# Cross-covariance attention: the V side moved one step further behind the attention

## The chip, the cores and the metric

The kernel runs on one core of a Trainium2 chip. The metric is device time in microseconds (us); a lower number is better. The kernel before was run five times: 131.57 to 134.93 us, median 132.96 us. One further execution was profiled; it took 131.79 us, and 130.0 us lie between its first and its last instruction (the span).

## The reference

Q, K and V have the shape 8 x 12 x 512 x 64 (batch, heads, sequence n, feature), float32. The attention is over features, not over the sequence, so each head has a 64 x 64 attention matrix:

```python
Q_norm = Q / (np.linalg.norm(Q, axis=-2, keepdims=True) + 1e-10)
K_norm = K / (np.linalg.norm(K, axis=-2, keepdims=True) + 1e-10)
attn = np.einsum('bhnd,bhne->bhde', Q_norm, K_norm)
attn = np.exp(attn - np.max(attn, axis=-1, keepdims=True))
attn = attn / (np.sum(attn, axis=-1, keepdims=True) + 1e-10)
return np.einsum('bhnd,bhde->bhne', V, attn).astype(np.float32)
```

## The kernel before, in words

The 96 heads are cut into 24 units of four heads (U = 24). For each unit Q and K are one transfer of 512 KB each (`load_qk`, L69 to L73). V comes in 12 transfers of 1024 KB, each for two units (`load_v`, L75 to L77). The output leaves in one transfer of 512 KB for each unit, the last unit in two halves (`store`, L79 and L80). All transfers are issued by SyncE, SP in the profile, on one queue, in the order in which the program names them.

One unit passes through these stages. VectorE (DVE) casts Q and K to bf16 side by side (`cast_q` L84, `cast_k` L87). TensorE (PE) makes their Gram matrix in 64 small matmuls (`grams` L103); it holds the product of Q and K and, on its diagonal, the squared norms. VectorE reads the norms (`norms` L115), GpSimd (POOL) takes the power of -1/2 (L120) and scales the part of K (`scale_k` L125), which ScalarE (ACT) copied out of PSUM before (`keep_kq` L108). PE transposes (`logits` L131), VectorE applies the norms of Q (`scale_q` L135), ScalarE takes the exponential (`exps` L139), VectorE divides by the row sums (`normalise` L143 to L147), and PE and ScalarE put the result into a second place as well (`doubled` L176 and L177).

The V side of unit v has three parts. `cast_v(v)` (L96) casts half of a V transfer to bf16, one half of that on ScalarE and the other on VectorE. `vtrans(v)` transposes it on PE (L155) and copies it out of PSUM on ScalarE (L159). `outs(v)` multiplies it by the attention matrix on PE (L188) and copies the product on ScalarE (L192). The last four units use `vtrans_f32` (L170, L171), which transposes V without a cast and shares the copies between ScalarE and VectorE.

The order is written out by hand, and the pools keep to it (`manual_schedule`). A loop over s = 0..23 runs steps. Step s names: the transfers of Q and K of unit s + 3, the V transfers and stores that fall due, `cast_v` for the units in `new`, `cast_q(s + 1)`, `normalise(s - 2)`, `grams(s)`, `norms(s)`, `keep_kq(s)`, `scale_k(s)`, `logits(s - 1)`, `scale_q(s - 1)`, `exps(s - 1)`, `cast_k(s + 1)`, `outs` for the units from n0 to n1, `doubled(s - 2)`, and last `vtrans` for the units in `new`. Each engine works its own instructions off in this order. `outs_by(s)` (L62 to L64) says how many units have had `outs` after step s; it sets the due times of all V work: V transfers are issued while fewer than (n1 + 5) // 2 have been, stores while fewer than n1 - 3 have been, and `new` reaches to n1 + 2. After the loop a tail runs the last six units: `vtrans_f32(u + 2)` and `outs(u)` for u = 18..23, with the rest of the attention of units 22 and 23 between them.

Buffers that matter: five for Q and K, four for V as it arrives (`vp`), three for V in bf16, ten for outputs, one PSUM buffer for the transposed V (`ps_v`), two for products (`ps_o`), and one for the Gram matrix, whose space is given to the tail's transposes once the loop is over.

Of the kernel before, what the change touches and what calls it, by code (L numbers as in the profile page):

```python
# [27 lines left out]
def kernel(  # L28
# [10 lines left out]
    U = B * H // HU  # L39
# [21 lines left out]

    def outs_by(s):  # L62

        return max(0, (s - 2) * 9 // 10)  # L64


    qf, kf, vf, vb, qkb, nsq, rq, kqs, sl, ex, vt, so, kq = ({} for _ in range(13))
# [7 lines left out]
    def load_v(w):  # L75
        vf[w] = vp.tile([128, 2 * R * D], F32, name="vf")
        nc.sync.dma_start(out=vf[w], in_=Vf[w])  # L77

    def store(u, g=slice(0, SV)):  # L79
        nc.sync.dma_start(out=Of[u][:, g], in_=so[u][:, g].rearrange("p s t d -> p s (t d)"))  # L80
# [8 lines left out]
    def cast_v(v):  # L89

        w, i = divmod(v, 2)
        if i == 0:
            vb[w] = vbp.tile([128, A, TP, 2 * D], BF16, name="vb")
        x = vf[w].rearrange("p (a t d) -> p a t d", a=A, d=2 * D)
        for t, copy in ((2 * i, nc.scalar.copy), (2 * i + 1, nc.vector.tensor_copy)):
            copy(vb[w][:, :, t], x[:, :, t])  # L96
# [52 lines left out]
    def vtrans(v):  # L149

        w, i = divmod(v, 2)
        ps = ps_v.tile([128, A, 2, 128], BF16, name="vps")
        for t in range(2):
            for a in range(A):
                nc.tensor.transpose(ps[:, a, t, :], vb[w][:, a, 2 * i + t, :], identb)  # L155

        if i == 0:
            vt[w] = vtp.tile([128, TP, 128, A], BF16, name="vt")
        nc.scalar.copy(vt[w][:, 2 * i:2 * i + 2], ps.rearrange("p a t c -> p t c a"))  # L159
# [19 lines left out]
    def outs(u, copies=(nc.scalar.copy, nc.scalar.copy)):  # L179
        s = so[u] = sop.tile([128, SV, TP, 2 * D], F32, name="so")  # L180
        a = abuf[u % len(abuf)]
        v = vt[u // 2][:, :, u % 2 * 64:(u % 2 + 1) * 64]
        for g in range(SV):
            po = ps_o.tile([128, TP, 2 * D], F32, name="po")
            for t in range(TP):
                for x in range(2):
                    h = 2 * g + x
                    nc.tensor.matmul(  # L188
                        po[MV * x:MV * (x + 1), t, :], v[:, t, NP * h:NP * (h + 1), :].rearrange("p c a -> p (c a)"),
                        a[:, h].rearrange("p a d -> p (a d)"), tile_position=(0, MV * x),  # L190
                    )
            copies[g](s[:, g], po)  # L192
# [21 lines left out]
    def clear(i):  # L214

        nc.scalar.copy(abuf[i].rearrange("p h a d -> p (h a d)"), zeros)
# [4 lines left out]
    def on(f, u):  # L221
        if 0 <= u < U:
            f(u)

    on(cast_q, 0)
    on(cast_k, 0)
    load_v(0)
    nv, nst, nt = 1, 0, 0
    for s in range(U):
        n0, n1 = outs_by(s - 1), outs_by(s)  # L230
        on(load_qk, s + LOAD_AHEAD)
        while nv < min(U, n1 + 5) // 2:
            load_v(nv)
            nv += 1
        while nst < n1 - 3:
            store(nst)
            nst += 1
        new = range(nt, n1 + 2) if s >= 1 else ()
        for v in new:
            cast_v(v)  # L240
        on(cast_q, s + 1)
        on(normalise, s - 2)
        on(grams, s)
        on(norms, s)
        on(keep_kq, s)
        on(scale_k, s)
        on(logits, s - 1)
        on(scale_q, s - 1)
        on(exps, s - 1)
        on(cast_k, s + 1)  # L250
        for v in range(n0, n1):
            outs(v)
        on(doubled, s - 2)
        if 6 <= s + 5 < len(abuf):
            clear(s + 5)
        for v in new:
            vtrans(v)
            nt = v + 1
# [59 lines left out]
```

## Time and profile before

| What | Value |
|---|---|
| median of 5 runs | 132.96 us (131.57 to 134.93) |
| profiled execution: time, span | 131.79 us, 130.0 us |
| mean granted PE clock | 0.835 of full speed |
| busy: PE, DVE, ACT, POOL | 89.7, 95.2, 91.5, 63.6 us |
| moved | 50.67 MB, mean 390 GB/s |
| from issue to landing: Q, K, V, output (median) | 11.5, 11.2, 12.6, 11.2 us |

The profile page gives each engine's busy time, the span in 40 slices of 3.25 us with a busy digit each, the queues, the chain of work that ended last, and groups of instructions. A line of the timeline gives an instruction's start and length in us, the engine, the source line, the operation and its operands, and in square brackets how long the engine sat idle before it and who released it. The table by stretch gives busy us and instruction counts of PE, its weight loads, DVE, ACT and POOL, then the granted PE clock, the share of the DMA engines and GB/s.

### The profile page before, as it was taken

How to read it: one execution, taken by the hardware profiler on the slowest of the kernel's cores; microseconds unless marked ns; L12 is line 12 of the kernel's file. 1: busy time of each engine (PE TensorE's matmuls, PEld its weight loads, DVE VectorE, ACT ScalarE, POOL GpSimd, SP SyncE). 2: the span in 40 equal slices, each digit the busy share in tenths (PEclk: the TensorE clock that was granted, in tenths of full speed). 3: DMA queues.
4: the chain of work that ended last, by engine and by line, in shares of the span. 5: the costliest groups of instructions: out<-in, count | busy, mean ns of one | idle time of the engine just before them, and what ended most of it. 6: DMA issues, size and time to landing. Idle time of an engine off the chain costs nothing.

```text
span 130.0 us, 5389 instructions
## 1 busy us (share of the span) xinstructions
PE 89.7 (69%) x2232; PEld 69.7 (54%) x2232; DVE 95.2 (73%) x366; ACT 91.5 (70%) x171; POOL 63.6 (49%) x57
## 2 busy tenths in 40 slices
PE   0147328479977759883995699765598499979640
PEld 0136226357855537662873587554486378767420
DVE  0450673989798995993978897997689597878840
ACT  7600373575999999895778387999489968887530
POOL 4005080895369753751738574579347627640000
PEclk9999999955599996897579856999959955999965
DMA  4999999999999999999999999999999999998775
GB/s 151 355 391 427 421 412 406 410 418 407 402 421 397 426 404 416 417 416 406 422 405 413 403 419 415 409 418 415 411 414 422 400 420 413 415 359 328 297 287 203
DMA packets 15208, 50.67 MB, mean 390 GB/s; under 512 B 1360, under 2 KB 1360, under 8 KB 13648
## 3 DMA queue, kind: packets, MB, share of 16 engines
q1 hardware_dynamic: 15184, 50.34, 97.1%
q8 instruction: 17, 0.28, 0.8%
q14 instruction: 7, 0.06, 0.1%
HBM read 37.75 MB, written 12.58 MB: 387 GB/s over the span
## 4 chain that ended last, share of the span: by engine, by line
PE 44%; ACT 14%; DVE 13%; issue 9%; DMA 8%; POOL 6%; SPq 2%; DVEq 0%; POOLq 0%; ACTq 0%
PE gram L103 17%; PE po L188 9%; DMA vf<-in_V_dram 8%; PE vps L155 7%; DVE scr L115 5%; POOL rq L120 5%; PE lgdup L131 4%; ACT vt L159 4%; ACT so L192 4%; PE lgdup L176 3%; PE vps L170 2%; DVE sl L135 2%; POOL kqs L125 1%; ACT kq L108 1%; DVE qkb L87 1%
## 5 line engine op out<-in xcount | busy, mean ns | idle before, releaser
L120 POOL TENSOR_TENSOR rq<-nsq,mhalf 128x4 f32<-128x4 f32 x24 | 47.4, 1975 | 49.7 <-DVE nsq L115 35.8
L103 PE MATMUL gram<-qkb 32*128 32x128 bf16 x1536 | 36.1, 256 | 16.8 <-DVE qkb L87 9.1
L103 PEld LDWEIGHTS <-qkb 32*128 32x128 bf16 x1536 | 29.7, 114 | 23.5 <-DVE qkb L87 12.1
L115 DVE CUSTOM_DVE_ANT_0 scr<-gram,ident 128x128 f32<-128x128 f32 x96 | 22.1, 284 | 13.1 <-PE gram L103 13.0
L192 ACT COPY so<-po 128x512 f32<-128x512 f32 x42 | 22.8, 588 | 1.6 <-PE po L188 1.0
L108 ACT COPY kq<-gram 64x256 f32<-64x256 f32 x24 | 8.8, 368 | 21.2 <-DVE nsq L115 20.9
L188 PE MATMUL po<-ab,vt 128*64 128x128 bf16 x384 | 20.1, 257 | 2.5 <-ACT vt L159 1.1
L159 ACT COPY vt<-vps 128x1024 bf16<-128x1024 bf16 x20 | 20.2, 1012 | 1.5 <-PE vps L155 1.1
L84 DVE CAST qkb<-qf 128x1024 bf16<-128x1024 f32 x24 | 16.3, 679 | 5.9 <-DMA qf<-in_Q_dram 5.9
L155 PE MATMUL vps<-identb,vb 128*128 128x128 bf16 x160 | 15.0, 249 | 5.9 <-ACT vb L96 2.9
L188 PEld LDWEIGHTS <-vt 128*64 128x64 bf16 x384 | 15.0, 132 | 7.3 <-issue 4.7
L155 PEld LDWEIGHTS <-vb 128*128 128x128 bf16 x160 | 11.1, 111 | 11.4 <-ACT vb L96 4.8
L87 DVE CAST qkb<-kf 128x1024 bf16<-128x1024 f32 x24 | 16.2, 676 | 0.5 <-DMA kf<-in_K_dram 0.5
L131 PE MATMUL lgdup<-ident,kqs 64*64 64x64 f32 x96 | 12.7, 270 | 4.8 <-POOL kqs L125 4.0
L125 POOL TENSOR_TENSOR kqs<-kq,rq 64x256 f32<-64x256 f32 x24 | 14.7, 612 | 1.9
L96 ACT CAST vb<-vf 128x512 bf16<-128x512 f32 x20 | 12.3, 621 | 4.4 <-DMA vf<-in_V_dram 4.4
L131 PEld LDWEIGHTS lgdup<-ident,kqs 64*64 64x64 f32 x96 | 7.8, 133 | 9.0 <-POOL kqs L125 5.8
L96 DVE CAST vb<-vf 128x512 bf16<-128x512 f32 x20 | 8.4, 424 | 5.5 <-DMA vf<-in_V_dram 5.5
L139 ACT ACTIVATE ex<-sl 64x256 f32<-64x256 f32 x24 | 10.0, 417 | 2.1 <-DVE sl L135 1.6
L176 PE MATMUL lgdup<-ab,identb 64*64 64x256 bf16 x24 | 7.4, 306 | 5.6 <-DVE sl L135 4.7
L147 DVE TENSOR_TENSOR ab<-ex,rinv 64x256 bf16<-64x256 f32 x24 | 10.4, 433 | 0.8
L135 DVE TENSOR_TENSOR sl<-lgdup,rq 64x256 f32<-64x256 f32 x24 | 9.9, 412 | 1.2 <-PE lgdup L131 1.1
(21 smaller groups left out, 60.0 us busy)
## 6 DMA issues: line engine op xcount, KB each, us to landing
qf<-in_Q_dram SPq DMA_DIRECT2D x24, 512.0 KB, 11.5
kf<-in_K_dram SPq DMA_DIRECT2D x24, 512.0 KB, 11.2
vf<-in_V_dram SPq DMA_DIRECT2D x12, 1024.0 KB, 12.6
out_dram<-so SPq DMA_DIRECT2D x23, 512.0 KB, 11.2
out_dram<-so SPq DMA_DIRECT2D x2, 256.0 KB, 3.0
```

The costliest lines, as they stand in the source:

```text
L84: nc.vector.tensor_copy(qkb[u][:, :, 0:D], qf[u])
L87: nc.vector.tensor_copy(qkb[u][:, :, D:], kf[u])
L96: copy(vb[w][:, :, t], x[:, :, t])
L103: nc.tensor.matmul(gbuf[:, h, 0:2 * D], x, x, start=(t == 0), stop=(t == R - 1), tile_position=(NV * h, 0))
L115: nc.vector.tensor_tensor_reduce(out=scr, in0=gbuf[:, h, 0:2 * D], in1=ident, scale=1.0, scalar=1e-20, op0=ALU.mult, op1=ALU.add, accum_ou ...
L120: nc.gpsimd.tensor_tensor(out=r, in0=n2, in1=mhalf, op=ALU.pow)
L125: nc.gpsimd.tensor_tensor(out=kk[D:], in0=kq[u][D:], in1=rq[u][D:, :, None].to_broadcast([D, HU, D]), op=ALU.mult,)
L131: nc.tensor.transpose(lg[:, h, :], kqs[u][D:, h, :], ident[D:, D:])
L155: nc.tensor.transpose(ps[:, a, t, :], vb[w][:, a, 2 * i + t, :], identb)
L159: nc.scalar.copy(vt[w][:, 2 * i:2 * i + 2], ps.rearrange("p a t c -> p t c a"))
L188: nc.tensor.matmul(po[MV * x:MV * (x + 1), t, :], v[:, t, NP * h:NP * (h + 1), :].rearrange("p c a -> p (c a)"), a[:, h].rearrange("p a d ...
L192: copies[g](s[:, g], po)
```

## The change

`outs_by(s)` counts from step 3 where it counted from step 2, so after step 4 every due time of the V side falls one step later than before. The first V transfer is issued after the Q and K transfers of the fourth unit (unit 3) where it was issued ahead of them; the second is issued in step 3, after those of unit 6, where it was issued in step 0. `cast_v` for units 0 and 1 moves from step 1 to steps 3 and 4, where it is named behind `cast_k` and no longer at the head of the step. From step 5 on it is at the head, as before. No arithmetic is changed. At the end of the loop 18 units have had `outs` and 20 have been transposed, with both kernels, and the tail is the same.

```diff
     def outs_by(s):
 
-        return max(0, (s - 2) * 9 // 10)
+        return max(0, (s - 3) * 9 // 10)
...
     on(cast_q, 0)
     on(cast_k, 0)
-    load_v(0)
-    nv, nst, nt = 1, 0, 0
+    nv, nst, nt = 0, 0, 0
     for s in range(U):
         n0, n1 = outs_by(s - 1), outs_by(s)
         on(load_qk, s + LOAD_AHEAD)
-        while nv < min(U, n1 + 5) // 2:
+        while nv < (min(U, n1 + 5) // 2 if s >= 3 else 1):
             load_v(nv)
             nv += 1
         while nst < n1 - 3:
             store(nst)
             nst += 1
-        new = range(nt, n1 + 2) if s >= 1 else ()
-        for v in new:
-            cast_v(v)
+        new = range(nt, max(0, min(s - 2, n1 + 2)))
+        if s > 4:
+            for v in new:
+                cast_v(v)
         on(cast_q, s + 1)
         on(normalise, s - 2)
         on(grams, s)
...
         on(cast_k, s + 1)
+        if s <= 4:
+            for v in new:
+                cast_v(v)
         for v in range(n0, n1):
             outs(v)
```

## The prediction, before the result was known

> **What bounds the kernel now.** I read the page's 40 slices first.
>
> ```profile
> ACT  7600373575999999895778387999489968887530
> PEclk9999999955599996897579856999959955999965
> DMA  4999999999999999999999999999999999998775
> GB/s 151 355 391 427 421 412 406 410 418 407 402 421 397 426 404 416 417 416 406 422 405 413 403 419 415 409 418 415 411 414 422 400 420 413 415 359 328 297 287 203
> ```
>
> The DMA engines are busy from the second slice to about 114 us, at some 412 GB/s, and only the last five slices (114 us on) fall off. So up to there a transfer lands when the bytes named ahead of it on the one queue have been moved. I count its place: MiB named up to its own end. One MiB takes 2.55 us. The engines still don't idle much: ACT is at nine tenths in the middle. Compute and transfers are nearly level, and the question is which of them a step waits for. The waits and DVE's timeline answer it; then the SP timeline with the landing times.
>
> ```profile
> DVE vb L96 <- DMA vf<-in_V_dram: 5.5, 2, 4.2
> ACT kq L108 <- DVE nsq L115: 20.9, 15, 4.0
> ```
>
> ```profile
> 103.31 0.49 DVE L96 CAST vb<-vf 128x512 bf16<-128x512 f32 x1 [1.35 <-DMA vf<-in_V_dram]
> ...
> 107.08 0.41 DVE L96 CAST vb<-vf 128x512 bf16<-128x512 f32 x1
> ```
>
> ```profile
> 90.36 0.42 SPq L77 DMA_DIRECT2D vf<-in_V_dram  x1
> ...
> 94.62 0.33 SPq L72 DMA_DIRECT2D qf<-in_Q_dram  x1
> ```
>
> DVE waits for V twice: 4.2 us for V0 at the start (until 14.18, with the casts of unit 2 behind it), and 1.35 us for V9 in step 21. V9 was issued at 90.36 and landed 12.9 us later, at 103.26 (place 38.5); Q of unit 23, issued at 94.62, landed 11.2 us later, at 105.82 (place 39.5). So after V9 the end follows a chain of engine work. ACT's timeline shows it, from step 22 to the tail:
>
> ```profile
> 110.84 0.37 ACT L108 COPY kq<-gram 64x256 f32<-64x256 f32 x1 [0.68 <-DVE nsq L115]
> 111.24 0.42 ACT L139 ACTIVATE ex<-sl 64x256 f32<-64x256 f32 x1
> 111.68 1.07 ACT L192 COPY so<-po 128x512 f32<-128x512 f32 x2
> 112.78 0.37 ACT L177 CAST ab<-lgdup 64x256 bf16<-64x256 f32 x1
> 113.17 1.01 ACT L159 COPY vt<-vps 128x1024 bf16<-128x1024 bf16 x1
> ```
>
> One such block takes 3.34 us (110.84 to 114.18), with a V cast of 0.62 ahead of it. Its first copy starts only when the norms are read. Then PE runs the tail almost without a gap: outs(18) at 115.65 on the timeline, the last output copy ends at 126.02, and 4.0 us of last transfers bring the 130.0. The table by stretch shows PE's clock (columns: busy us of PE, PEld, DVE, ACT, POOL, then clock):
>
> ```profile
> 46.15:49.56 3.41, 1.96 (x29) 1.39 (x29) 3.20 (x14) 3.29 (x8) 2.25 (x2) 1.00 1.01 398
> 49.56:52.97 3.41, 3.41 (x87) 2.84 (x84) 2.01 (x13) 2.82 (x6) 0.73 (x2) 0.50 1.04 412
> 100.80:104.20 3.40, 1.67 (x58) 1.17 (x56) 2.05 (x8) 3.27 (x7) 2.27 (x2) 1.00 1.01 395
> 104.20:107.60 3.40, 3.39 (x57) 2.61 (x53) 3.33 (x16) 2.16 (x5) 1.24 (x1) 0.50 1.03 420
> 111.04:114.45 3.41, 2.45 (x85) 1.88 (x80) 2.90 (x14) 3.29 (x7) 2.39 (x3) 1.00 1.05 421
> ```
>
> A stretch with PE busy for 1.67 or 1.96 of 3.41 us is followed by half clock; one with 2.45 is not, nor is 2.27 at 83.73. So the step lies between 0.58 (1.98 at 121.28, half clock after it) and 0.66 of a stretch. The tail before runs at full clock because the stretch ahead of it has 2.45.
>
> **What the Trainium skill says.** "TensorE: Matmul & The Clock Gate", Part 1: The HAM clock gate: the clock is half or full, set by activity in free-running windows of 3413 ns. The trace agrees: 0.50 or 1.00, in stretches of 3.4 us or multiples. "Perfetto Trace Analysis", Tensor Engine Instruction: ACT, DVE and GPSIMD work strictly in order. The trace agrees: cast_q(22) stood behind the V9 cast although its data had landed at 99.5. "DMA: Bandwidth & Descriptors", Queues, rings and completion order: each DMA engine takes descriptors in ring order. The landings above go by place.
>
> **The change part by part.** No instruction is added or removed: 20 bf16 V units, 4 of float32, 25 stores in both.
>
> *Start.* V0 moves behind Q and K of unit 3 (place 5 for 4), V1 behind units 4 to 6 (9 for 6). K of unit 2 lands at 11.7 (3.08 + 8.6). Without the V casts ahead, DVE does cast_q(2) at 10.4, the norms of unit 1 after its Gram (11.9), scale_q(0) and cast_k(2) by 13.9; Gram 2 starts near 14 where it was 19.77. At 4.1 to 4.3 us for a step, and with the moved casts (0.41 on DVE, 0.62 on ACT each; PE's transposes and the next Gram wait for them, about 1 us each time), Gram 6 starts near 32 where it was 36.58. Lead: 4 to 4.5 us. V0 (about 17.2) is wanted near 22: hidden by 5 us. V1 (27.3) is wanted near 26.5: about 1 us of wait, counted in.
>
> *Middle.* From step 7 each V transfer is wanted one step later and lands 2.55 us later, because one more unit of Q and K (1 MiB) is ahead of it. Q and K themselves land 0.5 to 1.5 MiB earlier (unit 23: place 38.5 for 40). Stores pass behind one unit of Q and K on SP's queue; those up to 15 are computed long before, so SP doesn't wait. Nothing moves on POOL's queue. The lead now meets the V landings: V7 at 85.4 (place 31.5) for a cast wanted at 88.41 - 4.1 = 84.3; V8 at 95.8 (35.5) for 98.14 - 3.0 = 95.1; so the lead is 2.3 at step 20. V9 is the one that sets the end: place 39.5 for 38.5, so **105.8** (Q of unit 23 had this place before), and it is wanted at the head of step 22. The engines would be there at 107.08 - 2.3 - 1.35 (the old wait) = 103.4. They wait 2.4 us. cast_q(23), normalise(20) and the norms of unit 22 stand behind that cast on DVE, and ACT's copies behind those norms. Step 22 begins 107.08 - 105.8 = **1.3 us earlier** than before.
>
> *End.* DVE from the head of step 22 to the norms: 107.08 to 109.08, and 109.82 to 110.75; without the wait for the Gram between, 2.93 us: 108.75. Before, ACT then ran one block and the tail followed. Now outs(17) and vtrans(19) lie in step 23, so ACT runs a block, a V cast, and a block: 0.09 + 3.34 + 0.04 + 0.62 + 0.03 + 3.34 = 7.46, ending at 116.2. outs(18) needs that last copy: 116.25, where it was 115.65. So the chain gains 1.3 and gives back 1.9: **+0.6 us**.
>
> *Clock.* Between 106 and 116.2 PE has, at full clock, logits 0.41 twice, outs 0.64 twice, doubled 0.28 twice, bf16 transposes 0.62 twice, Gram 1.07, float32 transposes 1.09: 6.06 of 10.2 us, 0.59 of the time, and 1.5 us idle just ahead of outs(18). That is at the lower edge of the step found above. So I expect half clock for one window in the tail, where PE is the engine waited for. Half clock costs a factor of 1.6 to 1.77 (outs 1.03 for 0.64, transposes 1.03 for 0.62, logits 0.63 for 0.41, Gram 1.89 for 1.07); at 1.65, 3.41 x (1 - 1/1.65) = **1.3 us**. Its bounds: 0 (no window falls there) and 2.7 (two windows). I take one, because two need PE still idle at half clock, and it then is busy throughout.
>
> *Sum* for the profiled execution: 130.0 + 0.6 + 1.3 = 131.9 us of span, 133.7 with what lies around it. On the median 132.96 + 1.9 = 134.9. The profiled one was 1.2 below the median, so I add the difference to the median.
>
> **Rivals.**
> *No half clock in the tail.* The windows run free, so they may fall so that none of them is under the step. Then only the chain is left: 132.96 + 0.6 = 133.6.
> *Faster: V9 doesn't hold.* If V9 lands at 103.4 or earlier, the lead goes through: outs(18) at 113.8, 1.8 earlier, so 131.2. The floor is V11, place 43.5 in both, 116.15, where its first transpose was at 118.39: 2.2 earlier at most. It needs V9 ahead of 105.2 for any gain and ahead of 103.9 for one per cent. For it: slices reach 427 GB/s, and PE may run through the tail with less. Against: 39.5 MiB stand in the order, and the DMA engines were never idle.
> *The stores come late.* outs(16) and outs(17) end at 110.8 and 114.9, where it was 108.24 and 112.78. The queue still holds V10 and V11 then, and landing takes 2.8 us at least, so 114.9 + 2.8 = 117.7 is ahead of the 120.3 at which store 17 landed before. If that cover is gone, one store, 1.3 us, comes on top of the sum: 136.2.
>
> **How the numbers follow.** Half clock in the tail 0.45 (134.9; own range 134.0 to 136.4), no half clock 0.28 (133.6), V9 not holding 0.22 (131.2), late stores 0.05 (136.2). One per cent, 1.3 us, is about what a measurement of this kernel can tell from no change. So faster 0.22, same 0.28, slower 0.50. The range goes from 131.1, which leaves out half of the faster case, to 136.6, where two half-clock windows would begin.
>
> **What would show it.** Right: Gram 2 near 14 us; DVE waits for V in steps 18, 20 and 22, the last until about 105.8; ACT without a gap from 108.8 to 116.2; outs(18) at 116.2; clock 0.50 within 112 to 122. Wrong: a step 22 that starts before 104, or a V9 cast without a wait; then the lead reaches the tail and the time falls.

## The result and the profile after

The changed kernel takes 132.43 us (median of 44 runs, 131.42 to 133.44), the kernel before, run beside it, 132.32 us (79 runs). The ratio is 1.0047, with a 95% interval from 1.0030 to 1.0063. It compares the fast executions alone: 35 of the 79 of the kernel before lie more than 1.5% above its fastest (up to 135.67 us), and one of the 44 of the changed kernel does, so the two medians over all executions lie closer together than the ratio says. On 132.32 us the ratio is 0.6 us more, with 0.4 and 0.8 as the ends. The profiled execution took 133.01 us with a span of 131.2 us, so it is one of the longer ones; before it was 131.79 and 130.0.

Of the page's slices, PE's clock and the rate after:

```profile
PEclk9999999999997799986999599995995996899997
GB/s 140 396 403 433 402 411 415 406 408 420 406 415 413 403 422 403 410 425 400 411 425 405 412 413 425 408 406 428 403 415 416 418 411 417 389 317 243 278 273 207
```

The transfers are as dense as before up to about 112 us. PE's clock is at nine tenths or more in the four slices from 115 to 128 us, where the prediction had put a stretch of half clock; PE's last matmul ends at 126.3. The two waits that carried the prediction are these after:

```profile
ACT kq L108 <- DVE nsq L115: 28.4, 17, 4.0
...
DVE vb L96 <- DMA vf<-in_V_dram: 5.3, 4, 2.7
```

The 4.2 us at V0 are gone, and most of the waits for V now lie near the end: 0.43 (V1), 0.89 (V7), 1.29 (V8) and 2.70 us (V9). In DVE's timeline the casts behind V8 and V9:

```profile
95.19 0.55 DVE L96 CAST vb<-vf 128x512 bf16<-128x512 f32 x1 [1.29 <-DMA vf<-in_V_dram]
...
106.13 0.43 DVE L96 CAST vb<-vf 128x512 bf16<-128x512 f32 x1 [2.70 <-DMA vf<-in_V_dram]
```

V9 was issued at 92.69 and landed 13.4 us later, at 106.1. ACT's timeline from there, the norms' release of its queue and the second block that the change put into step 23:

```profile
109.06 0.37 ACT L108 COPY kq<-gram 64x256 f32<-64x256 f32 x1 [2.31 <-DVE nsq L115]
...
113.60 0.37 ACT L108 COPY kq<-gram 64x256 f32<-64x256 f32 x1 [0.69 <-DVE nsq L115]
113.99 0.42 ACT L139 ACTIVATE ex<-sl 64x256 f32<-64x256 f32 x1
114.43 1.07 ACT L192 COPY so<-po 128x512 f32<-128x512 f32 x2
...
115.92 1.01 ACT L159 COPY vt<-vps 128x1024 bf16<-128x1024 bf16 x1
```

PE, in its timeline, starts most of outs(18) only at 116.99, behind that copy, and the tail's transposes then take 1.09 us, as before. First the kernel before, then the changed kernel:

```profile
115.65 0.64 PE L188 MATMUL po<-ab,vt 128*64 128x128 bf16 x16
116.22 1.09 PE L170 MATMUL vps<-ident,vf 128*128 128x128 f32 x8
```

```profile
110.63 1.89 PE L103 MATMUL gram<-qkb 32*128 32x128 bf16 x64
...
116.99 0.53 PE L188 MATMUL po<-ab,vt 128*64 128x128 bf16 x12 [1.17 <-ACT vt L159]
...
117.44 1.09 PE L170 MATMUL vps<-ident,vf 128*128 128x128 f32 x8
```

So outs(18) comes 1.3 us later in this profile, and the last output copy ends 1.0 us later (127.02 for 126.02). The table by stretch shows where the half clock went (columns as in the prediction):

```profile
105.78:109.19 3.41, 0.53 (x12) 0.47 (x13) 2.99 (x14) 0.84 (x3) 0.07 (x1) 1.00 1.04 420
109.19:112.60 3.41, 3.24 (x75) 2.55 (x75) 1.99 (x7) 3.31 (x7) 2.44 (x2) 0.50 1.04 416
112.60:116.01 3.41, 2.81 (x41) 2.14 (x40) 2.74 (x13) 2.62 (x7) 1.62 (x2) 1.00 0.84 332
```

PE was idlest while DVE waited for V9 (0.53 of 3.41 us). The half-clock stretch comes right behind that wait and ends at 112.6, ahead of the tail.

### The profile page after: what moved, and what is told of

Its sections match the earlier page's. It is cut to its first block, busy times and chain, and to the rows that moved or that the text cites. A ratio compares the mean times of both kernels' runs of the same rounds, so it can differ in the third digit from the quotient of the medians.

```text
span 131.2 us, 5391 instructions
## 1 busy us (share of the span) xinstructions
PE 87.4 (67%) x2232; PEld 67.3 (51%) x2232; DVE 96.3 (73%) x366; ACT 91.3 (70%) x171; POOL 64.3 (49%) x57
## 3 DMA queue, kind: packets, MB, share of 16 engines
q1 hardware_dynamic: 15184, 50.34, 96.1%
## 4 chain that ended last, share of the span: by engine, by line
DMA 50%; PE 18%; DVE 13%; ACT 11%; issue 3%; SPq 1%; ACTq 0%; DVEq 0%
DMA qf<-in_Q_dram 22%; DMA kf<-in_K_dram 18%; DMA vf<-in_V_dram 10%; PE gram L103 10%; DVE scr L115 6%; ACT so L192 3%; PE vps L155 3%; PE po L188 3%; ACT vt L159 2%; DVE qkb L87 2%; ACT ex L139 2%; PE vps L170 2%; ACT kq L108 1%; ACT vb L96 1%; DVE qkb L84 1%
## 5 line engine op out<-in xcount | busy, mean ns | idle before, releaser
L103 PEld LDWEIGHTS <-qkb 32*128 32x128 bf16 x1536 | 30.5, 116 | 21.0 <-DVE qkb L87 12.8
L188 PE MATMUL po<-ab,vt 128*64 128x128 bf16 x384 | 18.3, 229 | 5.6 <-ACT vt L159 2.9
L84 DVE CAST qkb<-qf 128x1024 bf16<-128x1024 f32 x24 | 17.2, 716 | 6.4 <-DMA qf<-in_Q_dram 6.4
L188 PEld LDWEIGHTS <-vt 128*64 128x64 bf16 x384 | 12.5, 114 | 10.0 <-ACT vt L159 4.5
L125 POOL TENSOR_TENSOR kqs<-kq,rq 64x256 f32<-64x256 f32 x24 | 15.2, 635 | 1.9
L131 PE MATMUL lgdup<-ident,kqs 64*64 64x64 f32 x96 | 11.9, 257 | 4.7 <-POOL kqs L125 4.5
L143 DVE TENSOR_REDUCE esum<-ex 64x4 f32<-64x256 f32 x24 | 9.7, 403 | 0.7 <-ACT ex L139 0.6
```

The lines of the kernel that those rows point to most:

```text
L84: nc.vector.tensor_copy(qkb[u][:, :, 0:D], qf[u])
L103: nc.tensor.matmul(gbuf[:, h, 0:2 * D], x, x, start=(t == 0), stop=(t == R - 1), tile_position=(NV * h, 0))
L125: nc.gpsimd.tensor_tensor(out=kk[D:], in0=kq[u][D:], in1=rq[u][D:, :, None].to_broadcast([D, HU, D]), op=ALU.mult,)
L131: nc.tensor.transpose(lg[:, h, :], kqs[u][D:, h, :], ident[D:, D:])
L188: nc.tensor.matmul(po[MV * x:MV * (x + 1), t, :], v[:, t, NP * h:NP * (h + 1), :].rearrange("p c a -> p (c a)"), a[:, h].rearrange("p a d ...
```

## The experiments

Two theories stood against each other. Theory 1: V9's landing sets the end, through DVE's norms and ACT's copies behind it, and the early lead is given back there. Its rivals: the bytes or the lag of the V side set the end whatever V9 does. Theory 2 is about the clock: which window is at half clock, and whether the tail ever is. All ratios are to the kernel before, run on the same chip; a difference from the changed kernel is that of two such ratios. The edits are against the changed kernel, that of the lag alone against the kernel before.

**V9 ahead of Q and K of unit 23.**

```diff
+        if s == U - 4:
+            load_v(nv)
+            nv += 1
         on(load_qk, s + LOAD_AHEAD)
```

> The changed kernel with one transfer moved: V9 is issued ahead of Q and K of unit 23 (place 38.5 in the order for 39.5). Theory 1, the landing of V9 sets the end through the engine chain behind it: V9 lands near 103.5 us, DVE no longer waits 2.7 us for it; Q of unit 23 is then late by about 1 us, so the end comes some 1.7 us earlier than in the changed kernel, ratio to the kernel before 0.992. Rival, the end is set by the ACT copies of one more V unit or by the bytes, and the V9 wait is hidden: no change, ratio 1.005.

Measured: 0.9946 (0.9915 to 0.9976), that is 1.3 us less than the changed kernel (0.9946 / 1.0047 = 0.990). DVE's timeline at the head of step 22:

```profile
104.14 0.41 DVE L96 CAST vb<-vf 128x512 bf16<-128x512 f32 x1
...
104.86 0.69 DVE L84 CAST qkb<-qf 128x1024 bf16<-128x1024 f32 x1 [0.30 <-DMA qf<-in_Q_dram]
```

The V9 cast begins without a wait, 2.0 us ahead of the changed kernel's. One transfer moved by 1 MiB turns the loss into a gain. Theory 1 holds, and its rival falls. Some of the 2.0 us is lost on the way: Gram 22 ran mostly at half clock (1.70 us), and the norms waited 0.50 us for it.

**The start alone**, with the old lag.

```diff
-        return max(0, (s - 3) * 9 // 10)
+        return max(0, (s - 2) * 9 // 10)
...
-        while nv < (min(U, n1 + 5) // 2 if s >= 3 else 1):
+        while nv < (min(U, n1 + 5) // 2 if s >= 1 else 1):
...
-        new = range(nt, max(0, min(s - 2, n1 + 2)))
-        if s > 4:
+        new = range(nt, max(0, min(s - 1, n1 + 2)))
+        if s > 3:
...
-        if s <= 4:
+        if s <= 3:
```

> The kernel before with only the start of the change: first V transfer behind unit 3, second behind unit 4, first V casts behind those of Q and K in steps 2 and 3, the lag of the V side as before. Theory 1: Gram of unit 2 near 14 us, a lead of 4 us, all of it given back at V9, which lands near 103.3 as before: ratio 1.000 within 0.003. Rival, the early lead is worth time and it is the longer lag that loses it: ratio 0.98 or less.

Measured: 1.0040 (1.0003 to 1.0076). The rival (0.98) is out; the lead is given back. The value lies a little above the 1.000 +- 0.003 that was expected. The profiled execution took 135.08 us, 2.5 above this run's median of 132.56, so its lines show what can happen and not what is usual. In DVE's and PE's timelines:

```profile
103.70 0.43 DVE L96 CAST vb<-vf 128x512 bf16<-128x512 f32 x1 [2.65 <-DMA vf<-in_V_dram]
...
116.46 1.97 PE L170 MATMUL vps<-ident,vf 128*128 128x128 f32 x8
```

DVE waited 2.65 us for V9, where it waited 1.35 us before: the lead became a longer wait. PE then was at half clock from 106.1 to 119.7 us, into the tail, where a set of float32 transposes took 1.97 us for 1.09. Its last output copy ended at 129.1, 3.1 us later than in the profile before. So what the prediction priced can happen, but of all the profiles taken only this one and that of the added Grams below have half clock between 115 and 122 us, and in the latter it reaches only the first set of the tail's transposes (1.35 us).

**The lag alone**, with the old start.

```diff
-        return max(0, (s - 2) * 9 // 10)
+        return max(0, (s - 3) * 9 // 10)
```

> The kernel before with only the longer lag: the due times of V one step later, start as before (V0 first, its casts at the head of step 1). Theory 1: without the lead the engines reach step 22 near 105.7 us, where V9 lands at 105.8 to 106.1, so there is nearly no wait and the end is that of the changed kernel: ratio 1.005, within 0.004. Rival, the start of the change is what costs: ratio 1.000. Rival, the start of the change pays for the lag: ratio 1.015 or more.

Measured: 1.0088 (1.0059 to 1.0117), at the upper edge of what was expected. DVE began step 22 at 106.65 and waited for no V at all in the last 50 us: without the lead it arrives 0.4 us after V9 has landed (106.22), and 0.5 us behind the changed kernel's cast. So the lag costs nearly 0.9%, and the start of the change wins about 0.4% of it back, although alone it cost 0.4%: the two do not add. Neither of the rivals with a number (1.000, or 1.015 and more) fits.

**Each V transfer from step 3 on ahead of Q and K of its step.**

```diff
-        on(load_qk, s + LOAD_AHEAD)
+        if s < 3:
+            on(load_qk, s + LOAD_AHEAD)
         while nv < (min(U, n1 + 5) // 2 if s >= 3 else 1):
             load_v(nv)
             nv += 1
+        if s >= 3:
+            on(load_qk, s + LOAD_AHEAD)
```

> The changed kernel with each V transfer from step 3 on issued ahead of the Q and K of its step (1 MiB earlier in the order). Theory 1: the waits of DVE for V7, V8 and V9 (0.9, 1.3 and 2.7 us in the changed kernel) go or shrink, Q and K land up to 2.5 us later and give some of it back; the end 1.5 to 2.2 us earlier than in the changed kernel, ratio to the kernel before 0.988 to 0.994. Rival, the bytes or the ACT copies set the end: ratio 1.005.

Measured: 0.9901 (0.9867 to 0.9935), as theory 1 said: 1.9 us less than the changed kernel. DVE's waits for V in its profile sum to 1.2 us, where they were 5.3; those for Q rose from 6.4 to 8.7. This is the lowest ratio of the study, below both kernels.

**More PE work in the V9 wait:** Gram 22 done three times over.

```diff
         on(grams, s)
+        if s == 22:
+            grams(s)
+            grams(s)
```

> The changed kernel with the 64 Gram matmuls of unit 22 done three times over in step 22 (the second and third time write the same values again), to keep PE busy while DVE waits for V9. In the profiled execution of the changed kernel the stretch of that wait (PE busy 1.17 of 3.41 us) was followed by half clock, under which Gram 23 took 1.89 us and ACT waited 0.69 us for its norms. Theory 2, this half clock is part of the loss: Gram 23 takes 1.07 us, the 0.69 us go, ratio to the kernel before 1.000 (changed kernel 1.0047). Rival, the clock plays no part because the ACT copies are the chain either way: 1.005. If the two added Grams (2.1 us) aren't hidden by the wait: 1.01 or more.

Measured: 1.0243 (1.0190 to 1.0295), the expectation for the case that the added work isn't hidden. (The 1.17 us above is of a stretch set about 1 us too early; in the one that ends where half clock begins, PE was busy for 0.53 us.) PE's timeline:

```profile
107.02 1.57 PE L103 MATMUL gram<-qkb 32*128 32x128 bf16 x98 [1.66 <-issue]
112.81 1.07 PE L103 MATMUL gram<-qkb 32*128 32x128 bf16 x64 [2.05 <-ACT ab L177]
```

Gram 23 did take 1.07 us, but PE paused 1.66 us amid the added matmuls for nothing that the profile shows, and then waited 2.05 us for ACT. Half clock came all the same, at 114 to 117 us. The run says nothing on the price of the clock; it failed as a test.

**The output copies of unit 17 on VectorE.**

```diff
-            outs(v)
+            outs(v, (nc.vector.tensor_copy, nc.vector.tensor_copy) if s == U - 1 else (nc.scalar.copy, nc.scalar.copy))
```

> The changed kernel with the two output copies of unit 17, the only ones in step 23, on VectorE in place of ScalarE. Theory 1, after V9 the end goes through ACT's copies, and the V unit that the change put into step 23 costs there what its copies take: 1.07 us off ACT, some of it back on DVE, so the end comes 0.6 to 1.1 us earlier than in the changed kernel, ratio 0.997 to 1.000. Rival, PE's or DVE's order sets the tail: no change, 1.005, or slower.

Measured: 0.9986 (0.9948 to 1.0023), 0.8 us less than the changed kernel, as theory 1 said. The ACT copies of the V unit that the change put into step 23 do lie on the path.

**Both of these at once:** V transfers ahead, and the copies on VectorE.

> Both at once: each V transfer from step 3 on ahead of Q and K of its step, and the output copies of unit 17 on VectorE. If both costs lie on one chain they add: 0.990 less 0.005, so 0.984 to 0.987. If the last stores, which the version with only the transfers moved already had queued behind each other (landing 3.4 to 6 us after issue where 2.8 is the least), are the next limit, it stays at 0.988 to 0.990.

Measured: 0.9935 (0.9909 to 0.9961). The two do not add; the result is no better than with the transfers alone. The list of transfers fits that: the last half store lands 5.0 us after its issue, where the changed kernel's took 3.2. First the run with both, then the changed kernel:

```profile
out_dram<-so SPq DMA_DIRECT2D x1, 256.0 KB, 5.0
```

```profile
out_dram<-so SPq DMA_DIRECT2D x1, 256.0 KB, 3.2
```

The last copy ended at 123.57, but the stores stand behind each other until 128.6, and from 122 to 126 us the DMA engines moved 388 GB/s without a pause. So the bytes are the next limit in this profile; no run tested it apart.

**The old lag with the new start and V one step earlier** from step 8 on.

The edits of the start alone, with this line in place of theirs:

```diff
-        while nv < (min(U, n1 + 5) // 2 if s >= 3 else 1):
+        while nv < (min(U, n1 + (6 if s >= 8 else 5)) // 2 if s >= 1 else 1):
```

> The lag of the kernel before, the changed kernel's start (as in the run with the start alone), and from step 8 on each V transfer one step earlier, so that V9 stands at place 37.5 and V11 at 43. Theory 1: V9 (near 101 us) no longer holds the engines, so the lead of the start reaches the tail, where V11 near 115 us and the bytes limit it: 1.5 to 2.5 us earlier than the kernel before, ratio 0.981 to 0.989. Rival, the lead is worth nothing anywhere, or Q and K pushed back by the earlier V take it all: 0.998 or more.

Measured: 0.9945 (0.9921 to 0.9970), faster than before but short of the 0.981 to 0.989 expected. In the stretch from 85 to 112 us DVE now waits 4.1 us for Q (twice, up to 2.1 us). V9 in fact stood at place 37.0 and landed at 99.6, but Q of unit 22 fell from place 37 to 38 and landed at 102.1, where it was 99.6. The wait moved; it didn't go.

**The changed kernel profiled twice more.**

> The changed kernel once more, for a second profile of where PE's half clock falls. The prediction put one half-clock window (3.4 us) into the tail, at 1.3 us. Theory 2: the window that follows the V9 wait (PE idlest there) is the one at half clock, it is over before outs(18), and the tail runs at full clock, as in the first profile. Rival: the window falls freely, and in this profile part of the tail (116 to 122 us) is at half clock, with float32 transposes of about 2 us in place of 1.09.

> The changed kernel a third time, as the run before it: by theory 2 the tail at full clock again and the V9 wait of DVE at 2.2 to 2.9 us; by the rival a half-clock window within 116 to 122 us in about half of the profiles.

DVE's V9 wait was 2.65 and 2.07 us, and V9's cast began at 106.63 and 106.41. In both the tail ran at full clock from 116 us on. In the first, half clock lay at 108 to 115 us, right behind the wait, and ACT waited the same 0.69 us. In the second it lay at 101 to 107.5, around the wait. The second's timeline, PE and ACT:

```profile
110.39 1.07 PE L103 MATMUL gram<-qkb 32*128 32x128 bf16 x64
...
113.21 0.37 ACT L108 COPY kq<-gram 64x256 f32<-64x256 f32 x1
```

With Gram 23 at full clock there is no wait at the copy. outs(18) follows at 116.60; in the other two it is 116.99 and 117.49. Theory 2 holds for the tail in three profiles of three; that the window always follows the wait does not hold. Two more profiles are few: by the rival's own odds, half clock in about half of them, both would miss it one time in four.

## Why the prediction was right and where it failed

*The start: right.* Gram 2 began at 13.97 us (predicted: near 14) and Gram 6 at 32.52 (near 32).

*V9 sets the end: right, and shown.* The casts waited for V7, V8 and V9 in steps 18, 20 and 22; the landings read off the profile before (85.4, 95.8, 105.8) were met at 85.2, 95.2 and 106.1 in the first profile, and in the other two at 85.5, at 96.1 and 96.2, and at 106.6 and 106.4. Moving V9 alone took 1.3 us out.

*The chain behind V9: right in its path, rough in its size.* The norms released ACT at 109.06 (108.75). ACT's two blocks end at 116.93, where 116.2 was written; of the difference 0.3 is V9's later landing, and the rest is the 0.69 us at Gram 23 less a somewhat tighter chain. The copies on VectorE showed that the second block is on the path. The whole term was +0.6 us. In the three profiles outs(18) came 1.34, 1.84 and 0.95 us later than before, and the last output copy 1.0, 1.5 and 0.6 us later.

*The clock: wrong. This is the step that failed:* "So I expect half clock for one window in the tail, where PE is the engine waited for", at 1.3 us. In all three profiles of the changed kernel the tail ran at full clock, and the term is 0 there. Two things in it were wrong.

The first is the mean. The activity of PE was averaged over the whole 106 to 116.2 us, and the window was put behind the last idle piece. But PE is idlest in the V9 wait itself. In two of the three profiles half clock came right behind that wait, under ACT's copies, where the dearer Gram 23 cost 0.69 us; in the third it lay around the wait and cost nothing there. From V9's landing to outs(18) it is 10.88 and 10.89 us in the two, and 10.22 in the third.

The second is the step of 0.58 to 0.66, read from a few stretches. It does not hold in the later profiles. The third profile of the changed kernel has, just ahead of and into outs(18), the stretch that was feared, with PE busy for 0.52 of it. Full clock follows:

```profile
114.38:117.79 3.41, 1.79 (x27) 1.37 (x26) 1.90 (x5) 3.14 (x7) 0.00 (x0) 1.00 0.85 332
117.79:121.20 3.41, 3.41 (x52) 2.66 (x51) 2.61 (x6) 2.67 (x6) 0.00 (x0) 1.00 0.82 309
```

The run with V9 ahead has the same at 113.49 to 116.90 (1.79 us, full clock behind it). In the second profile of the changed kernel a stretch of 1.81 us (97.72 on) is followed by full clock and one of 1.84 us (104.55 on) by half. So PE's busy time alone does not tell.

Nor does a stretch that PE fills always end the half clock, as the bound against a second window took it. In the profile before, half clock went on behind such a stretch (3.39 us, 104.20 to 107.60):

```profile
107.60:111.04 3.44, 3.44 (x87) 2.86 (x85) 2.63 (x14) 2.71 (x6) 2.12 (x3) 0.50 1.03 410
```

In the start-alone run it lasted for four stretches. What decides it is open, and so is why the tail of the changed kernel was spared.

*The sum.* Without that term the sum is 132.96 + 0.6 = 133.6, the first rival, or a ratio of 1.0045; measured 1.0047. That it fits so closely is partly luck: V9 landed 0.3 to 0.8 us later than written, half clock cost 0.69 us at Gram 23 in two profiles of three, and the way from outs(18) to the last copy, 0.3 us shorter than before, made up for some of it. The direction was right; the measured change is a third of the size forecast. Two small slips changed nothing: the half-clock factor of the logits is 1.54 (0.63 for 0.41), below the range given, and two windows in the tail would give 136.3, not 136.6.

*The rivals.* V9 did hold, so the faster case did not come; the run with V9 ahead shows what such a landing is worth, 1.3 us. Stores 16 and 17 were issued at 110.99 and 115.53 (written: 110.8 and 114.9), and they did no harm: the last ones landed about 3 us after issue, as before.

What stays open: why the start alone came out at 1.004 rather than 1.000. A longer V9 wait leaves PE idle for longer and half clock behind it, which would fit; so would V9 itself, which landed 0.4 us later in that run's profile than before (103.67 for 103.28, at the same place). No run tells them apart.

## What to carry to other kernels

With one queue that is full all the time, a transfer's landing can be read from the profile before to within about 1 us (here 0.8 at most): find what had the same place in the order. A head start of the engines is worth only what the latest transfer in the order lets through, so ask of each moved load what it is now behind, and who stands behind its first user. Don't price a changing clock by a mean over a long stretch, and before you use a threshold read from a few stretches, try it on all stretches of the traces at hand; where it fails, give the clock a range and not a place.

## What the runs showed of the hardware

Half clock on PE came in stretches of 3.41 us, alone or up to four in a row (106.1 to 119.7 us in the start-alone run). No threshold on PE's busy time comes out of these traces: stretches of 0.53 and 1.84 us were followed by half clock, stretches of 1.79 and 1.81 us by full clock. At the start the record of the clock reads 1.00 while the 64 matmuls of a Gram take 1.89 us, their length at half clock, and not 1.07: in the kernel before up to Gram 2 at 19.77, in the changed kernel up to Gram 5 at 28.51. So the record there does not show the speed, and the mean clock of a profile comes out too high.

PE paused for 1.66 us within a plain run of matmuls, with no releaser in the profile, in the run with the added Grams; the kernel before has such pauses too, 1.26 us of it in Gram 21.
